# Token sums of an FFN on GpSimd, and one slot of row products moved to the end

## The chip, the cores and the metric

One core of a Trainium2 chip runs one launch of the kernel. The metric is the device time of the launch in microseconds, from repeated executions. The core's engines are TensorE (PE, matrix products), VectorE (DVE), ScalarE (ACT), GpSimd (POOL) and SyncE (SP), each with its own in-order queue; weights come by DMA.

## What is computed

A decoder trunk of two layers on 512 tokens of 1024 features, in float32. Layer 0 mixes tokens by dilated window attention, layer 1 by a gated linear recurrence. Each is followed by a gated FFN with a causal convolution of three taps; the change is in this part, which runs twice.

```python
D_MODEL = 1024; SEQ = 512; D_FF = 3 * D_MODEL

def conv_ffn(x, w_up, conv_w, conv_b, w_down):
    u = causal_dwconv(x @ w_up, conv_w, conv_b)
    g, v = u[..., :D_FF], u[..., D_FF:]
    return (jax.nn.gelu(g, approximate=True) * v) @ w_down

# in reference(), after the token mixer of each layer:
    h = rms_norm(x, norm_ffn_pre[layer])
    h = conv_ffn(h, ffn_w_up[layer], ffn_conv_w[layer], ffn_conv_b[layer], ffn_w_down[layer])
    x = x + rms_norm(h, norm_ffn_post[layer])
```

## The kernel before

**Precision.** Every operand of a product is kept as two float32r tiles, a high part `hi` (a rounding copy on ScalarE, L149) and a low part `lo` (the rest, a subtraction on VectorE, L150). A product is three matmuls: hi by hi, hi by lo, lo by hi (`PASSES`). The normed activations of a layer are `hT`, turned so that features lie on the partitions: two tiles of 128 x 8 x 512.

**An FFN.** `ffn` first takes the feature tiles of j = 0 and 1 as plain products (`feat_tiles`, `tiles`): 8 half tiles and 4 whole ones on TensorE, each followed by a tick. The other ten j (`SEVEN`) go through `seven`: for each j and each half (gate and value) one chain, twenty in all. A chain computes 256 features by seven block products in place of eight, from sums of blocks of weights on one side and of `hT` on the other. The sums of `hT` over halves of features and tokens are made once per FFN by `token_sums`: `both` adds hi and lo of a part of `hT` (L938, 128 x 512 elements), `whole` does it for the two parts of a block, the blocks `b11`, `b12`, `b22`, `b21` are combined on VectorE (L956, L963, L944) and split into the tiles `T[0]` to `T[3]` (`parted`).

**Slots.** A chain occupies a cycle of ten slots (`CYCLE`). `AT` says at which slot of its cycle a chain's step stands: step 1 at 0, 5 at 1, 2 at 2, 6 at 4, 3 at 5, 7 at 8, and 4 at 13, in the next chain's cycle. A step is twelve matmuls of 256 columns. Steps 5, 6, 7 and 4 multiply by `T[0]`, `T[1]`, `T[2]` and `T[3]`, the others by `hT`. A step accumulates in a PSUM bank that an earlier step wrote, so step 6 waits for the copy (L1031) of what step 1 left, step 3 for the copy after step 5, step 7 for the copy after step 6, and step 4 for an addition on VectorE that follows step 7 (L1040). The taps of the convolution are L777.

The slots that `free_slots` lists lie between the steps. They hold products of the second FFN matrix for the rows k = 0 to 19, two slots a row, six matmuls of 512 columns each (`rows`); with twenty chains there are forty. Slots that hold nothing are skipped.

**Order by hand.** The order on every engine is the order in which the program emits instructions. `slot` emits a step, then what is due (`later(n, f)` puts f behind n more slots), then `tick`: one step of every side generator, and `pump`, which converts the next weight piece to hi and lo (one piece per slot in `seven`, while at most 16 halves live). `token_sums` is such a side generator: each `yield n` lets n ticks pass. It is started five ticks into the FFN. `stream` lists the weight pieces of the chains by due times: the pieces `w11`, `s1`, `w12`, `s2`, `s3`, `s4`, `a22` of each chain, the additions between blocks of a weight tile (`left` and `ahead` as accumulating DMAs of GpSimd at L186, `across` at L210 and `lower` at L214 on VectorE), and for each row k its weight (`rows`, loaded by SyncE 16 slots before use) and its activation (`act`).

At its start `token_sums` also sends the residual stream to DRAM by a GpSimd DMA (L922), because its SBUF place becomes the home of `T`. The same function serves the attention stage with `first=True`, where it does not touch the residual stream.

Before an FFN the tokens are normed in four blocks t (`norms`, `prenorm`): products with gain and root on VectorE (L481, L485), transposition on TensorE (L502) and the split into `hT` (L506 on ScalarE, L507 on VectorE). The last block is still on its way when the first products of the FFN run.

Of the kernel before, what the change touches and what calls it, by code (L numbers as in the profile page):

```python
# [11 lines left out]
F32 = mybir.dt.float32  # L12
# [3 lines left out]
ALU = mybir.AluOpType  # L16
# [25 lines left out]
CYCLE = 10  # L42
# [41 lines left out]
def kernel(  # L84
# [25 lines left out]
    nc = tc.nc  # L110
# [12 lines left out]
    def nm(s):  # L123
        uid[0] += 1
        return f"{s}{uid[0]}"

    def gen(dt=F32, s="g"):
        return gp.tile([P, 512], dt, tag="g", name=nm(s))
# [19 lines left out]
    def split(hi, lo, raw):  # L148
        nc.scalar.activation(hi, raw, AF.Copy)  # L149
        nc.vector.tensor_tensor(lo, raw, hi.bitcast(F32), op=ALU.subtract)  # L150
# [41 lines left out]
    def free_slots(n):  # L192

        end = CYCLE * n
        free = [CYCLE * c + r for c in range(n) for r in ((6, 7) if c > 1 else (7,))] + [end, end + 1]
        assert not {CYCLE * c + a for c in range(n) for a in AT.values()} & set(free)
        return free

    def stream(i0, n):

        items = []
        for c in range(n):
# [15 lines left out]
            for at, item in (  # L218
# [4 lines left out]
                if isinstance(item[0], str):  # L223
                    item = ((i, item[0]), lambda i=i, h=item[1]: [blocks(i)[h]], item[0] == "a22")
                items.append((o + at, item))
        free = free_slots(n)
        direct = up["direct"]
        at = 0
# [535 lines left out]
    def ffn(layer, hT, post, pre):  # L764
# [63 lines left out]
        up["direct"] = direct  # L828
        T = []
        side(token_sums(hT, T), 5)  # L830
        for j in range(SEVEN[0]):
            if j:
# [84 lines left out]
    def token_sums(hT, T, first=False):  # L917

        if not first:
            assert len(sides) == 1, len(sides)  # L920
            d = dp.tile([P, 4, D], F32, name=nm("x_kept"))
            nc.gpsimd.dma_start(d, X[0])  # L922
            kept.append(d)
        homes = cp.tile([P, 4, D], F32R, tag="x_sb", name=nm("T"))
        homes = [homes[:, n] for n in range(4)]
        homes += [cp.tile([P, D], F32R, tag="gain", name=nm("T"), bufs=2) for _ in range(1 if first else 2)]
        homes = [[h[:, 0:512], h[:, 512:1024]] for h in homes]
        if first:
            homes += [[gen(F32R, "T") for _ in range(2)]]
        homes += [[wp.tile([P, 512], F32R, tag=t, name=nm("T")) for _ in range(2)] for t in ("hi", "lo")]  # L930
        state["live"] += 2
        homes = [[h.rearrange("p (k t) -> p k t", k=2) for h in hs] for hs in homes]
        yield 1 + first

        def both(k0, n):
            o = gen(s="B").rearrange("p (k t) -> p k t", k=2)
            hi, lo = (h[:, k0 : k0 + 2, n * 256 : n * 256 + 256] for h in hT)
            tt(o, hi.bitcast(F32), lo.bitcast(F32), op=ALU.add)  # L938
            return o

        tt = nc.vector.tensor_tensor

        def negative(o, a, b):
            nc.vector.scalar_tensor_tensor(o, a, -1.0, b, op0=ALU.mult, op1=ALU.subtract)  # L944

        def whole(k0, n):
            return [both(k0 + 2 * k, n) for k in range(2)]

        def parted(n, b):
            for k in range(2):  # L950
                split(homes[2 * n][k], homes[2 * n + 1][k], b[k])

        b11, b12 = whole(0, 0), whole(0, 1)
        yield 1 + first
        for k in range(2):
            tt(b11[k], b11[k], b12[k], op=ALU.subtract)  # L956
        parted(0, b11)
        yield 1 + first
        b22 = whole(4, 1)
        if not first:  # L960
            yield 1
        for k in range(2):
            tt(b12[k], b22[k], b12[k], op=ALU.subtract)  # L963
            negative(b22[k], b11[k], b22[k])
        yield 1 + first
        parted(1, b22)
        T.extend([homes[2 * n], homes[2 * n + 1]] for n in range(4))
        yield 1 + first
        parted(2, b12)
        yield 1 + first  # L970
        b21 = whole(4, 0)
        if first:
            yield 2
        for k in range(2):
            negative(b21[k], b22[k], b21[k])
        yield 1 + first
        parted(3, b21)
# [68 lines left out]
    def seven(hT, T, begin, prep):  # L1046
# [25 lines left out]
        for j in SEVEN:  # L1072
            for half in range(2):
                f = chain(right, *ends(j, half))
                steps.update((CYCLE * n + AT[p], f(p)) for p in AT)
                n += 1
        free = free_slots(n)
        assert len(free) == len(fill)
        steps.update(zip(free, fill))
# [12 lines left out]
    def attention(hT, post, pre):  # L1092
# [359 lines left out]
        for hp in range(4):  # L1452
            q, k = [], []
            if hp % 2 == 0:
                v = []
                values(v) if hp else first_values(v)
            if hp == 0:
                side(build)
                side(token_sums(hT, T, True), 2)
            sink = qk_sink(q, k)  # L1460
            if hp < 3:
                feat_tiles(2, hT, sink)
                for hh in range(2):
                    side(local(2 * hp + hh, hh, q, k, v), 1 + hh)
# [252 lines left out]
```

## Time and profile before

| | |
|---|---|
| median of 3 runs | 1430.48 us (1429.96 to 1431.25) |
| the profiled execution | 1431.97 us |
| its span, first to last instruction | 1430.1 us |
| mean granted clock of TensorE | 0.994 |
| busy: PE, DVE, ACT, POOL | 98%, 80%, 56%, 16% |
| plain products of the first FFN begin, its chains begin | 489.3 us, 535.9 us |
| the same in the second FFN | 1035.1 us, 1081.7 us |

Times in the profile are microseconds from the span's start, unless marked ns. A row of a timeline has the start, the duration, the engine, the line, the operation, what it writes and reads (by tile names, with buffer numbers left out), the form and the count, and in brackets the idle time of the engine ahead of it and what ended it. A row of the waits view has who waited and for whom, the sum, the number of times and the longest. The profile is one execution; matmul ends are modelled. Names ending in q are sequencers.

### The profile page before, as it was taken

The page shows a single profiled execution, that of the slowest core. Times are in us where ns is not written, and L with a number is a line of the kernel's source. Part 1 is how long each engine was busy: PE and PEld are TensorE (multiplying, and loading weights), DVE is VectorE, ACT ScalarE, POOL GpSimd, SP SyncE. Part 2 cuts the span into 40 slices and gives each one's busy share as a digit, 9 for nine tenths or more (in the row PEclk, how much of TensorE's full clock was granted, in tenths as well). Part 3 has the DMA queues.
Part 4 walks back from the last instruction along what each step waited for, and adds up shares of the span by engine and source line. Part 5 has one row for each costly group of instructions (what it writes and reads, how often), then busy time and mean ns, then how long its engine had stood idle before and what let it go on. Part 6 is the DMA issues. An engine that isn't in the chain of part 4 may idle for free.

```text
span 1430.1 us, 23824 instructions
## 1 busy us (share of the span) xinstructions
PE 1405.7 (98%) x8885; PEld 1275.0 (89%) x8885; DVE 1140.5 (80%) x2229; ACT 800.2 (56%) x1670; POOL 235.4 (16%) x352
## 2 busy tenths in 40 slices
PE   9999999999999998999999999999998999999997
PEld 7888999999998888999999889888897999999886
DVE  6676898787855988988888758779789898888843
ACT  7343555363636555666666555588455656666641
POOL 0341333130400211222110001000101112211000
PEclk9999999999999999999999999999999999999999
DMA  7553455664756545666664632432354666665511
GB/s 225 180 146 105 131 166 151 171 178 144 190 171 218 167 116 108 153 155 148 148 125 119 221 118 89 134 117 89 119 155 93 137 147 155 147 151 119 183 57 59
DMA packets 176108, 204.03 MB, mean 143 GB/s; under 512 B 10688, under 2 KB 145304, under 8 KB 175736
## 3 DMA queue, kind: packets, MB, share of 16 engines
q1 hardware_dynamic: 123064, 153.34, 33.5%
q0 software_dynamic: 52080, 48.11, 18.7%
q8 instruction: 70, 1.15, 0.3%
q10 hardware_dynamic: 848, 1.05, 0.2%
q14 instruction: 46, 0.38, 0.1%
HBM read 183.51 MB, written 18.96 MB: 142 GB/s over the span
## 4 chain that ended last, share of the span: by engine, by line
PE 84%; DVE 9%; ACT 5%; issue 1%; DMA 1%; POOL 0%; DVEq 0%; SPq 0%; ACTq 0%
PE ps L1022 38%; PE acc L412 24%; PE ps L412 9%; PE v L1215 7%; DVE wlo L150 2%; DVE u L777 2%; PE v L1153 1%; DVE xb L1520 1%; ACT whi L149 1%; PE O L1427 1%; PE S L1361 1%; PE S L1309 1%; DVE B L938 1%; ACT sig L1541 1%; PE tr L502 1%
## 5 line engine op out<-in xcount | busy, mean ns | idle before, releaser
L150 DVE TENSOR_TENSOR wlo<-raw,whi 128x512 fp32r<-128x512 f32 x632 | 417.5, 686 | 111.8 <-ACT whi L149 109.0
L149 ACT ACTIVATE whi<-raw 128x512 fp32r<-128x512 f32 x632 | 371.3, 625 | 141.9 <-PE ps L1022 45.9
L1022 PE MATMUL ps<-T,whi 128*128 128x256 f32 x1792 | 329.6, 284 | 14.8 <-ACT part L1031 11.0
L1022 PEld LDWEIGHTS ps<-T,whi 128*128 128x128 f32 x1792 | 280.6, 191 | 20.6 <-ACT part L1031 11.4
L1022 PE MATMUL ps<-T,wlo 128*128 128x256 f32 x896 | 252.0, 281 | 0.0
L1022 PE MATMUL ps<-hT,whi 128*128 128x256 f32 x1344 | 250.1, 284 | 0.0
L412 PE MATMUL ps<-hT,whi 128*128 128x512 f32 (+1 forms) x960 | 248.3, 348 | 0.0
L1022 PEld LDWEIGHTS ps<-hT,whi 128*128 128x128 f32 x1344 | 210.7, 192 | 0.8
L1022 PE MATMUL ps<-hT,wlo 128*128 128x256 f32 x672 | 190.9, 284 | 0.0
L412 PEld LDWEIGHTS ps<-hT,whi 128*128 128x128 f32 x960 | 167.6, 189 | 22.2
L186 POOL DMA_DIRECT2D raw<-in_ffn_w_up_dram x80 | 102.9, 1312 | 455.5 <-DVE wlo L150 337.2
L1022 PEld LDWEIGHTS ps<-T,wlo 128*128 128x128 f32 x896 | 171.5, 191 | 0.0
L412 PE MATMUL ps<-hT,wlo 128*128 128x512 f32 (+1 forms) x480 | 166.4, 347 | 0.0
L412 PE MATMUL acc<-whi,ahi 128*128 128x512 f32 x352 | 137.4, 390 | 0.0
L412 PE MATMUL acc<-whi,alo 128*128 128x512 f32 x352 | 137.2, 390 | 0.2
L412 PE MATMUL acc<-wlo,ahi 128*128 128x512 f32 x352 | 137.0, 389 | 0.0
L1022 PEld LDWEIGHTS ps<-hT,wlo 128*128 128x128 f32 x672 | 129.5, 193 | 0.0
L1031 ACT ACTIVATE part<-ps 128x256 f32<-128x256 f32 x168 | 63.8, 380 | 96.1 <-PE ps L1022 91.1
L1215 PE MATMUL v<-whi,hT 128*128 128x512 f32 x320 | 106.5, 396 | 0.0
L412 PEld LDWEIGHTS ps<-hT,wlo 128*128 128x128 f32 x480 | 90.8, 189 | 11.4
L777 DVE SCALAR_TENSOR_TENSOR u<-ps,cols,u 128x511 f32<-128x511 f32 x112 | 83.6, 746 | 4.9 <-ACT u L773 2.9
L773 ACT ACTIVATE u<-ps,cols 128x512 f32<-128x512 f32 x56 | 43.5, 776 | 70.8 <-DVE ps L1035 64.5
(206 smaller groups left out, 2165.3 us busy)
## 6 DMA issues: line engine op xcount, KB each, us to landing
raw<-in_ffn_w_up_dram SPq DMA_DIRECT2D x48, 1024.0 KB
raw<-in_attn_w_qkv_dram SPq DMA_DIRECT2D x67, 512.0 KB
raw<-in_ffn_w_up_dram POOLq DMA_DIRECT2D x80, 256.0 KB, 4.8
raw<-in_ffn_w_down_dram SPq DMA_DIRECT2D x14, 1024.0 KB
dw<-in_ffn_w_down_dram SPq DMA_DIRECT2D x40, 256.0 KB
raw<-in_lru_w_in_dram SPq DMA_DIRECT2D x8, 1024.0 KB
turned<-T POOLq DMA_DIRECT2D x26, 256.0 KB, 2.6
ft<-turned POOLq DMA_DIRECT2D x104, 64.0 KB, 4.4
```

Source lines behind the costliest of these rows:

```text
L149: nc.scalar.activation(hi, raw, AF.Copy)
L150: nc.vector.tensor_tensor(lo, raw, hi.bitcast(F32), op=ALU.subtract)
L186: nc.gpsimd.dma_start(to, src, accum_op=ALU.add)
L412: mm(dst, l[a], r[b], start=start and n == 0, stop=stop and n == 2)
L502: nc.tensor.transpose(ps[:, k * P : (k + 1) * P], xs[i][:, k * P : (k + 1) * P], ident)
L773: nc.scalar.activation(u, ps, AF.Identity, scale=own[:, j : j + 1], bias=cc[:, 48 + j : 49 + j])
L777: nc.vector.scalar_tensor_tensor(u[:, d:], ps[:, : S - d], wc, u[:, d:], op0=ALU.mult, op1=ALU.add)
L938: tt(o, hi.bitcast(F32), lo.bitcast(F32), op=ALU.add)
L1022: mm(dst, W[wa][0][:, k, :], right[n](ha, k), start=n in (1, 5) and k == q == 0, stop=k == 3 and q == 2, skip_group_check=True,)
L1031: later(1, lambda: nc.scalar.activation(to, dst, AF.Copy))
L1153: mm(banks[t], hT[a][:, k, t * P : (t + 1) * P], W[b][k % 2][:, 0, :], start=u == n == 0, stop=u == 3 and n == 5,)
L1215: mm(bank, hT[a][:, k, t * P : (t + 1) * P], W[b][k % 2][:, 0, :], start=(k, a, b) == (0, 0, 0), stop=(k, a, b) == (KD - 1, 1, 0),)
```

## The change

In `token_sums`, for the FFNs alone (`first` is false): all four blocks `b11`, `b12`, `b22`, `b21` are now added up at the generator's first step, and the eight additions run on GpSimd in place of VectorE, queued behind the DMA of L922. The generator's first `yield` and one later `yield` go, one becomes `yield 2`: the combinations of `b11` and `b12` keep their tick, all that follows comes one tick earlier. The attention stage keeps its order and engine.

In `free_slots`, the third cycle (slots 20 to 29) has one free slot in place of two, slot 27, and slot `end + 2`, which is 202, is added. The forty products of rows keep their order, so each from the third on takes the next slot of the list. The due times of the row weights and activations in `stream` are computed from the same list.

```diff
     def free_slots(n):
 
         end = CYCLE * n
-        free = [CYCLE * c + r for c in range(n) for r in ((6, 7) if c > 1 else (7,))] + [end, end + 1]
+        free = [CYCLE * c + r for c in range(n) for r in ((6, 7) if c > 2 else (7,))] + [end, end + 1, end + 2]
...
         homes = [[h.rearrange("p (k t) -> p k t", k=2) for h in hs] for hs in homes]
-        yield 1 + first
+        if first:
+            yield 2
 
         def both(k0, n):
             o = gen(s="B").rearrange("p (k t) -> p k t", k=2)
             hi, lo = (h[:, k0 : k0 + 2, n * 256 : n * 256 + 256] for h in hT)
-            tt(o, hi.bitcast(F32), lo.bitcast(F32), op=ALU.add)
+            (nc.vector if first else nc.gpsimd).tensor_tensor(o, hi.bitcast(F32), lo.bitcast(F32), op=ALU.add)
             return o
...
         b11, b12 = whole(0, 0), whole(0, 1)
-        yield 1 + first
+        if not first:
+            b22, b21 = whole(4, 1), whole(4, 0)
+        yield 2
         for k in range(2):
             tt(b11[k], b11[k], b12[k], op=ALU.subtract)
         parted(0, b11)
         yield 1 + first
-        b22 = whole(4, 1)
-        if not first:
-            yield 1
+        if first:
+            b22 = whole(4, 1)
         for k in range(2):
             tt(b12[k], b22[k], b12[k], op=ALU.subtract)
             negative(b22[k], b11[k], b22[k])
@@
         yield 1 + first
         parted(2, b12)
         yield 1 + first
-        b21 = whole(4, 0)
         if first:
+            b21 = whole(4, 0)
             yield 2
         for k in range(2):
             negative(b21[k], b22[k], b21[k])
```

## The prediction

> **What bounds the kernel now.** I read the page's busy times first, then the waits of TensorE, then the timelines around each wait.
>
> ```profile
> PE 1405.7 (98%) x8885; PEld 1275.0 (89%) x8885; DVE 1140.5 (80%) x2229; ACT 800.2 (56%) x1670; POOL 235.4 (16%) x352
> ...
> PE ps L1022 <- ACT part L1031: 11.0, 2, 5.5
> ...
> PE ps L1022 <- DVE ps L1040: 3.8, 3, 1.3
> ```
>
> TensorE is busy 98% of the span, so only its waits, or a slower clock, can be won. The waits view has two large ones: 5.5 us, twice, on a copy that ScalarE makes (L1031). Of the three on L1040, two lie in the stages that the change touches. TensorE's timeline shows the places:
>
> ```profile
> 545.78 0.80 PE L1022 MATMUL ps<-T,whi 128*128 128x256 f32 x2 [5.49 <-ACT part L1031]
> ...
> 552.05 0.39 PE L412 MATMUL acc<-whi,whi 128*128 128x512 f32 x1
> ...
> 552.74 0.40 PE L1022 MATMUL ps<-T,whi 128*128 128x256 f32 x2
> ...
> 799.05 0.39 PE L1022 MATMUL ps<-T,whi 128*128 128x256 f32 x1 [1.29 <-DVE ps L1040]
> ...
> 1091.61 0.80 PE L1022 MATMUL ps<-T,whi 128*128 128x256 f32 x2 [5.49 <-ACT part L1031]
> ...
> 1345.02 0.39 PE L1022 MATMUL ps<-T,whi 128*128 128x256 f32 x1 [1.28 <-DVE ps L1040]
> ```
>
> Each FFN shows the same pair: 5.49 us at slot 4 of the twenty chains (step 6 of the first chain), and 1.29 us before the very last step. The first one costs more than its length, as the windows view of L1022 tells (the stretch and its length, busy time and count of matmuls, the same of weight loads, granted clock, DMA share, GB/s):
>
> ```profile
> 545.77:551.70 5.93, 5.49 (x24) 5.20 (x24) 0.50 0.43 138
> ...
> 552.70:562.70 10.00, 9.96 (x84) 9.95 (x84) 1.00 0.91 199
> ```
>
> After the idle stretch the clock is 0.50. At clock 1.00 a matmul takes 10.00/84 = 0.119 us, a step of twelve 1.43 us; six row products take 2 x (552.74 - 552.05) = 1.38 us. From 545.78 to 552.74 there lie 24 step matmuls and six row products: 2 x 1.43 + 1.38 = 4.24 us at full clock, 6.96 measured. The slow clock costs 2.72 us, so that the wait costs 8.21 us per FFN. After the 1.29 us wait nothing of the kind is seen.
>
> What is late? ScalarE's timeline, then VectorE's:
>
> ```profile
> 513.89 0.62 ACT L149 ACTIVATE whi<-raw 128x512 fp32r<-128x512 f32 x1
> ...
> 514.42 0.76 ACT L773 ACTIVATE u<-ps,cols 128x512 f32<-128x512 f32 x1
> ...
> 543.70 1.23 ACT L149 ACTIVATE T<-B 128x512 fp32r<-128x512 f32 x2 [4.95 <-DVE B L944]
> ...
> 545.36 0.36 ACT L1031 ACTIVATE part<-ps 128x256 f32<-128x256 f32 x1
> ...
> 548.52 1.15 ACT L149 ACTIVATE whi<-raw 128x512 fp32r<-128x512 f32 x2 [2.00 <-DVE raw L210]
> ...
> 549.58 0.36 ACT L1031 ACTIVATE part<-ps 128x256 f32<-128x256 f32 x1
> ```
>
> ```profile
> 500.06 1.29 DVE L507 TENSOR_TENSOR hT<-tr,hT 128x512 fp32r<-128x512 f32 x2 [0.23 <-ACT hT L506]
> ...
> 501.27 3.69 DVE L150 TENSOR_TENSOR wlo<-raw,whi 128x512 fp32r<-128x512 f32 x6
> ...
> 506.43 1.53 DVE L777 SCALAR_TENSOR_TENSOR u<-ps,cols,u 128x511 f32<-128x511 f32 x2 [1.47 <-ACT u L773]
> ...
> 510.52 1.29 DVE L150 TENSOR_TENSOR wlo<-raw,whi 128x512 fp32r<-128x512 f32 x2 [2.56 <-ACT whi L149]
> ...
> 511.74 1.53 DVE L777 SCALAR_TENSOR_TENSOR u<-ps,cols,u 128x511 f32<-128x511 f32 x2
> ...
> 513.18 2.49 DVE L938 TENSOR_TENSOR B<-hT,hT 128x512 f32<-128x512 f32 x4
> ...
> 515.59 0.69 DVE L150 TENSOR_TENSOR wlo<-raw,whi 128x512 fp32r<-128x512 f32 x1
> ...
> 523.73 1.29 DVE L938 TENSOR_TENSOR B<-hT,hT 128x512 f32<-128x512 f32 x2
> ...
> 541.78 1.28 DVE L938 TENSOR_TENSOR B<-hT,hT 128x512 f32<-128x512 f32 x2
> ```
>
> The copy at 545.36 stands in ScalarE's queue behind the split of the fourth token sum (543.70), which waited 4.95 us for VectorE. From 511.74 on VectorE's rows show no idle time until the wait is over; four, two and two of the instructions in its queue are the adds of L938. The start is bound by VectorE's queue.
>
> **The adds leave VectorE.** Four adds hold it from 513.18 to 515.59, 2.41 us or 0.60 each; eight are 4.8 us. Not all of it comes through. Without the first four, VectorE would come at 513.18 to the low part (515.59), whose high part ScalarE ends at 513.89 + 0.62 = 514.51, and then to taps whose input ends at 514.42 + 0.76 = 515.18: about 1.4 us of idle time opens. Net, the queue runs 3.4 us earlier.
>
> **The token sums come a slot earlier.** With one yield less, the splits of the fourth sum no longer stand behind the last tile's taps and conversions, but the copy needed by step 7 (549.58) still stands behind a split that waits for L210. It gets the 3.4 us alone: it ends at 549.94 - 3.4 = 546.5. Where TensorE goes on at 545.78 - 5.49 = 540.29 without a wait at step 6, it stands before step 7 at 540.29 + 1.43 + 1.43 + 1.38 = 544.53. So the wait moves from step 6 to step 7 and is 2.0 us. I take the clock to stay at 1.00, since 2.0 is nearer to the 1.29 us row than to the 5.49 us row. Step 7 begins at 546.5 in place of 552.74: 6.2 us per FFN, which is the 8.2 of now less the 2.0 that remain.
>
> In the rule of the Trainium skill (TensorE: Matmul & The Clock Gate, Part 1: The HAM clock gate) the clock halves after about 3.4 us without work; by it too a wait of 2.0 us leaves the clock alone.
>
> **What GpSimd pays, and what it may take back.** No add of this size runs on GpSimd in this trace. Its own queue has room:
>
> ```profile
> 495.75 0.57 POOL L922 DMA_DIRECT2D x_kept<-x_sb  x1 [5.42 <-DVE x_sb L580]
> ...
> 516.57 2.63 POOL L186 DMA_DIRECT2D raw<-in_ffn_w_up_dram  x2 [20.25 <-DVE wlo L150]
> ...
> 531.22 2.58 POOL L186 DMA_DIRECT2D raw<-in_ffn_w_up_dram  x2 [12.02 <-DVE wlo L150]
> ...
> L1105 POOL COPY row<-rb 8x1 f32<-8x1 f32 x6 | 0.8, 177 | 0.1
> ...
> L1105 POOL COPY row<-rb 8x30 f32<-8x30 f32 x2 | 0.4, 201 | 0.0
> ```
>
> The adds are queued between 495.75 and 516.57, ahead of the accumulating DMAs that wait for VectorE anyhow. Two may begin at 496.3, as the first half of the tokens is complete; the others wait for the last tokens (500.06 + 1.29 = 501.35). A copy costs 24/29 = 0.83 ns an element, so an add of 512 costs 0.60 us if both reads go side by side, 1.03 us if one follows the other; as an estimate from these rows I take 1.03, and 2.06 as the upper end. Six adds from 501.35 end by 507.5, or 513.7: ahead of the first use, which VectorE reaches at about 517 (518.36 now):
>
> ```profile
> 518.36 1.28 DVE L956 TENSOR_TENSOR B<-B,B 128x512 f32<-128x512 f32 x2
> ...
> 530.24 1.29 DVE L150 TENSOR_TENSOR wlo<-raw,whi 128x512 fp32r<-128x512 f32 x2
> ```
>
> So GpSimd's slowness itself costs nothing. What may cost is work of VectorE beside it. Where GpSimd issues DMAs (531.22), VectorE's pair at 530.24 takes the usual 1.29 us, so the lower end is 0. The upper end is that the six low parts from 501.27, each reading two SBUF tiles, wait for an add in turn: five adds between six instructions, 5 x 1.03 less the 1.47 us idle row behind them, 3.7 us per FFN. Another collision can come earlier:
>
> ```profile
> 497.54 0.88 DVE L485 TENSOR_SCALAR xs<-xs,s 128x512 f32<-128x512 f32 x2
> ...
> 498.80 0.38 PE L502 MATMUL tr<-ident,xs 128*128 128x128 f32 x2
> ```
>
> These scalings end 0.4 us before TensorE transposes their results, and the first two adds would run beside them. I take 1.0 us per FFN in all, one add's hold-up: nearer to the DMA row than to the alternation.
>
> **The moved slot.** Six matmuls move from slot 26 to slot 202; their count is unchanged. At the end, TensorE gets 1.38 us of work between slots 201 and 203, while what step 4 waits for (L1040, behind step 7 at slot 198) does not move. That covers the 1.29 us. In the third cycle eight steps then follow as closely as they already do in the first two, where, besides step 6, the waits view shows nothing. From slot 27 on each weight conversion is issued one slot later against its use: the shortest lead, that of s4, goes from seven slots to six, over 8 us. The order of conversions stays: row weights and activations still lie between s2 and s3 of their chain, though L214 now precedes them and the SP loads of the row weights come one slot later, fifteen slots before use. One more half lives (14 of 16). I cost this at nothing; the leads hide it, and if they did not, each late slot would show as a TensorE wait.
>
> **Sum.** Per FFN: -6.2 (start) - 1.3 (end) + 1.0 (GpSimd beside VectorE) = -6.5 us; two FFNs, -13.0 us. The profiled execution took 1431.97 us, a span of 1430.1 and 1.9 around it; it would take 1419.0. It stood 1.5 us above the median of 1430.48, so the forecast is **1417.5 us**.
>
> **Rivals.**
>
> *VectorE and GpSimd alternate.* Every two-tile instruction of VectorE waits for the add in flight. The queue is late by 3.7 us; step 6 waits 3.7 and step 7 2.0. Per FFN -8.2 + 5.7 - 1.3 = -3.8, in all -7.6: 1422.9 us. For it: six such instructions lie just where the adds run. Against: no row shows GpSimd's work stretching one. Chance 0.25.
>
> This is the rule of the Trainium skill (SBUF — State Buffer, Who interferes with whom): an instruction of VectorE with two SBUF inputs and a GpSimd instruction that reads SBUF exclude each other for the whole instruction; no overlap of the two is in this trace. GPSIMD Engine Reference, Performance versus the Vector engine, states 4497 ns for 2048 elements, an estimate of 1.1 to 1.25 us for 512; with 1.25 the sum by this rival would be near 1426.5.
>
> *The same, with slow adds: slower.* With an add of length a, step 6 waits 5a - 1.47, and where that is near 5.49 again the clock falls too (+2.72), whose slower steps hide the wait at step 7. Against 8.21 + 1.29 it breaks even at a = (8.21 + 1.29 - 2.72 + 1.47)/5 = 1.65 us. At the upper end, 2.06, it is 8.83 + 2.72 - 9.50 = +2.05 per FFN, +4.1: 1434.6 us. Chance 0.12.
>
> *The start does not gain.* The copy stays behind ScalarE work that follows TensorE's tiles, not VectorE, and the adds bring nothing; the end slot alone gives -2.6: 1427.9 us. Against it: the 4.95 us row names VectorE. Chance 0.08.
>
> **How the numbers follow.** My own case has 0.52, and 0.03 is left for others. A measurement can tell some 0.2%, 2.9 us, from no change. Faster: 0.52 + 0.25 + 0.02 = 0.79; same: 0.08 + 0.01 = 0.09; slower 0.12. The range goes from 1414.5 (no collision at all, -15.0, and a little more at step 7) to 1428.0, which holds the alternation and the end slot alone, and leaves out the slower case.
>
> **What would show it.** Right: eight adds on GpSimd per FFN, in the first one between 496 and 512, no L938 on VectorE but the first stage's eight; no 5.49 us wait, one of about 2 us at step 7; clock 1.00 throughout; no L1040 wait at the ends. Wrong: the six low parts after 501 spread over 8 us or more; a wait of over 4 us with the clock at 0.50; or new TensorE waits from the third cycle on.

## The result: no change that can be measured

| | before | after |
|---|---|---|
| median, lowest and highest of 12 runs each | 1430.56 us (1429.51 to 1433.91) | 1430.45 us (1430.00 to 1431.60) |
| ratio after to before, 95% interval | | 0.9998 (0.9989 to 1.0007) |
| profiled execution, its span | 1431.97 us, 1430.1 us | 1430.45 us, 1428.7 us |

The forecast was 1417.5 us. In the profile after, step matmuls are L1024, the copy that step 6 waits for is L1033, the addition behind step 7 is L1042, and all additions of `both` are L939. First the page's busy times and the waits of TensorE:

```profile
PE 1405.0 (98%) x8885; PEld 1273.9 (89%) x8885; DVE 1147.4 (80%) x2213; ACT 800.4 (56%) x1670; POOL 260.0 (18%) x368
...
PE ps L1024 <- ACT part L1033: 10.3, 3, 4.9
PE tr L502 <- DVE xs L485: 3.3, 2, 1.7
...
PE ps L1024 <- DVE ps L1042: 1.1, 1, 1.1
```

Two readings. VectorE has 16 instructions fewer than before (2213 against 2229) and is busy 6.9 us longer (1147.4 against 1140.5). Sixteen additions of 0.60 us, 9.7 in all, left it, so the others grew by 16.6 us; where an instruction that is held up counts as busy, that is how a hold-up looks. And the long wait is still there, shorter by little, with a new one of 1.7 us on the scalings L485. Of the waits on the addition behind step 7, the two at the ends of the FFNs are gone; the one left lies in the attention stage. TensorE's timeline:

```profile
500.42 1.09 PE L502 MATMUL tr<-ident,xs 128*128 128x128 f32 x8 [1.66 <-DVE xs L485]
...
546.86 0.79 PE L1024 MATMUL ps<-T,whi 128*128 128x256 f32 x2 [4.88 <-ACT part L1033]
...
553.86 0.40 PE L1024 MATMUL ps<-T,whi 128*128 128x256 f32 x2
...
1092.50 0.79 PE L1024 MATMUL ps<-T,whi 128*128 128x256 f32 x2 [4.88 <-ACT part L1033]
...
1098.92 0.50 PE L1024 MATMUL ps<-T,whi 128*128 128x256 f32 x2 [0.55 <-ACT part L1033]
```

Step 7 begins at 553.86, where it began at 552.74. The windows view has the slow clock behind the wait as before. Its columns here: the stretch and its length; busy time and count of TensorE, its weight loads, VectorE, ScalarE and GpSimd; granted clock, DMA share, GB/s:

```profile
546.86:550.20 3.34, 3.34 (x15) 3.34 (x16) 3.34 (x6) 0.74 (x2) 0.00 (x0) 0.50 0.00 0
550.30:553.69 3.39, 3.39 (x16) 3.12 (x16) 3.29 (x7) 1.43 (x3) 1.02 (x1) 0.62 0.39 103
```

Then what GpSimd and VectorE did at the FFN's start. GpSimd's timeline, its group of additions over both FFNs, and VectorE's timeline:

```profile
495.56 0.57 POOL L922 DMA_DIRECT2D x_kept<-x_sb  x1 [5.40 <-DVE x_sb L580]
496.14 2.55 POOL L939 TENSOR_TENSOR B<-hT,hT 128x512 f32<-128x512 f32 x2
502.84 9.80 POOL L939 TENSOR_TENSOR B<-hT,hT 128x512 f32<-128x512 f32 x6 [4.15 <-DVE hT L507]
...
L939 POOL TENSOR_TENSOR B<-hT,hT 128x512 f32<-128x512 f32 x16 | 24.7, 1576 | 8.3 <-DVE hT L507 8.3
```

```profile
495.18 0.68 DVE L481 TENSOR_TENSOR xs<-x_sb,gain 128x512 f32<-128x512 f32 x1
...
496.03 3.21 DVE L481 TENSOR_TENSOR xs<-x_sb,gain 128x512 f32<-128x512 f32 x1
...
499.87 0.88 DVE L485 TENSOR_SCALAR xs<-xs,s 128x512 f32<-128x512 f32 x2
...
500.88 2.48 DVE L507 TENSOR_TENSOR hT<-tr,hT 128x512 fp32r<-128x512 f32 x4
503.28 9.92 DVE L150 TENSOR_TENSOR wlo<-raw,whi 128x512 fp32r<-128x512 f32 x6
513.12 1.52 DVE L777 SCALAR_TENSOR_TENSOR u<-ps,cols,u 128x511 f32<-128x511 f32 x2
```

The six low parts, 3.69 us before, take 9.92 beside six additions. The additions too are held up: the first two, beside which VectorE's product stood still, take 2.55 us, 1.3 each, but six take 9.80, so from one to the next it is (9.80 - 1.30) / 5 = 1.70 us. The two engines take turns. Earlier, the product L481 takes 3.21 us: it stood through both of the first additions. Before, its row was this:

```profile
496.23 0.68 DVE L481 TENSOR_TENSOR xs<-x_sb,gain 128x512 f32<-128x512 f32 x1
```

L777 comes at 513.12, where it came at 506.43.

To set the runs side by side, three distances, read from TensorE's timeline in both FFNs: from the start of the first transposition to that of the last one ("norms"), from there to the start of step 7 of the first chain ("start"), from there to the end of the twenty chains ("chains"). The first FFN stands ahead of the second.

| | norms | start | chains | median, us |
|---|---|---|---|---|
| before | 16.6, 16.6 | 53.2, 53.3 | 248.0, 248.0 | 1430.56 |
| after | 18.5, 18.5 | 52.6, 52.0 | 246.5, 246.6 | 1430.45 |

The norms lose 1.9 us per FFN, the start gains 0.6 and 1.3, the chains gain 1.5 and 1.5. Together that is -1.1 us; the span shrank by 1.4.

### The profile page after: what moved, and what is told of

Same layout as the page of the kernel before. It is cut to its first block, busy times and chain, and to the rows that moved or that the text cites. A ratio compares the mean times of both kernels' runs of the same rounds, so it can differ in the third digit from the quotient of the medians.

```text
span 1428.7 us, 23886 instructions
## 1 busy us (share of the span) xinstructions
PE 1405.0 (98%) x8885; PEld 1273.9 (89%) x8885; DVE 1147.4 (80%) x2213; ACT 800.4 (56%) x1670; POOL 260.0 (18%) x368
## 4 chain that ended last, share of the span: by engine, by line
PE 48%; DVE 11%; ACT 5%; issue 2%; DMA 0%; DVEq 0%; ACTq 0%
PE ps L1024 27%; PE acc L412 20%; DVE wlo L150 3%; DVE xb L1522 1%; DVE u L777 1%; ACT whi L149 1%; PE ps L412 1%; ACT sig L1543 1%; DVE x_sb L580 1%; DVE post L575 1%; DVE T L150 1%; DVE hT L507 0%; ACT sig L1562 0%; ACT a L1560 0%; ACT xhi L149 0%
## 5 line engine op out<-in xcount | busy, mean ns | idle before, releaser
L150 DVE TENSOR_TENSOR wlo<-raw,whi 128x512 fp32r<-128x512 f32 x632 | 432.2, 705 | 125.2 <-ACT whi L149 121.0
L1024 PE MATMUL ps<-T,whi 128*128 128x256 f32 x1792 | 329.5, 284 | 11.4 <-ACT part L1033 10.3
L1024 PEld LDWEIGHTS ps<-T,whi 128*128 128x128 f32 x1792 | 280.7, 191 | 16.9 <-ACT part L1033 11.1
L1024 PE MATMUL ps<-T,wlo 128*128 128x256 f32 x896 | 252.0, 281 | 0.0
L1024 PE MATMUL ps<-hT,whi 128*128 128x256 f32 x1344 | 249.3, 284 | 0.0
L1024 PEld LDWEIGHTS ps<-hT,whi 128*128 128x128 f32 x1344 | 210.0, 192 | 0.8
L1024 PE MATMUL ps<-hT,wlo 128*128 128x256 f32 x672 | 190.4, 283 | 0.0
L1024 PEld LDWEIGHTS ps<-T,wlo 128*128 128x128 f32 x896 | 171.5, 191 | 0.0
L1024 PEld LDWEIGHTS ps<-hT,wlo 128*128 128x128 f32 x672 | 129.0, 192 | 0.0
L1033 ACT ACTIVATE part<-ps 128x256 f32<-128x256 f32 x168 | 63.4, 378 | 79.2 <-PE ps L1024 78.3
L777 DVE SCALAR_TENSOR_TENSOR u<-ps,cols,u 128x511 f32<-128x511 f32 x112 | 83.5, 745 | 2.0
L455 POOL DMA_DIRECT2D turned<-T x34 | 18.6, 549 | 350.3 <-DVE T L449 348.7
```

The source lines that it names most:

```text
L455: nc.gpsimd.dma_start(d, T)
L777: nc.vector.scalar_tensor_tensor(u[:, d:], ps[:, : S - d], wc, u[:, d:], op0=ALU.mult, op1=ALU.add)
L1024: mm(dst, W[wa][0][:, k, :], right[n](ha, k), start=n in (1, 5) and k == q == 0, stop=k == 3 and q == 2, skip_group_check=True,)
L1033: later(1, lambda: nc.scalar.activation(to, dst, AF.Copy))
```

## The experiments

Theory A is the forecast's rival of alternation: an instruction of VectorE with two tiles from SBUF and an addition on GpSimd exclude each other. Theory B: the moved slot costs in the third cycle what it gains at the end. Theory C: ScalarE or TensorE's tiles hold the start, whoever adds. Theory D: any work of GpSimd holds up VectorE. The code cuts are against the kernel after, except that of e9_fill, which is against the kernel before. Line numbers below an edit differ from run to run: the copy that step 6 waits for stands nine lines below the step matmuls, the addition behind step 7 eighteen.

**e1_slot: the slot alone.** The change with `token_sums` as before, all its yields included.

```diff
-        if first:
-            yield 2
+        yield 1 + first
...
-            (nc.vector if first else nc.gpsimd).tensor_tensor(o, hi.bitcast(F32), lo.bitcast(F32), op=ALU.add)
+            tt(o, hi.bitcast(F32), lo.bitcast(F32), op=ALU.add)
...
```

> The slot moved alone, the additions on VectorE as before. Theory A (two reads exclude each other: a VectorE instruction that reads two SBUF tiles and a GpSimd addition cannot run at the same time, and what the moved slot wins is lost by this): the wait of 1.29 us before the last step goes in both FFNs, the 5.49 us wait stays, 2.6 to 3.2 us faster than before. Rival B (the moved slot itself costs in the third cycle what it wins at the end): no faster than before, and a new TensorE wait behind slot 27.

Measured: 1428.32 us, ratio 0.9983 (0.9974 to 0.9992). The waits view keeps the start as before and has no wait at the ends:

```profile
PE ps L1022 <- ACT part L1031: 11.0, 2, 5.5
...
PE ps L1022 <- DVE ps L1040: 1.1, 1, 1.1
```

The chains take 246.5 us in both FFNs, as after. The median fell by 2.2 us; the expected 2.6 to 3.2 lies within the interval (1.1 to 3.7 us). The slot does what was forecast, and theory B falls.

**e2_adds: the additions alone.** The change with `free_slots` as before.

```diff
-        free = [CYCLE * c + r for c in range(n) for r in ((6, 7) if c > 2 else (7,))] + [end, end + 1, end + 2]
+        free = [CYCLE * c + r for c in range(n) for r in ((6, 7) if c > 1 else (7,))] + [end, end + 1]
```

> The additions on GpSimd alone, the slots as before. Theory A: the two waits at the transposition (1.7 us) and the wait at step 6 (4.9 us, clock at 0.50 behind it) as with the whole change, and the 1.29 us at the end again: 2 to 3.5 us slower than before. Rival B: 0 to 3 us faster than before.

Measured: 1433.72 us, ratio 1.0024 (1.0014 to 1.0034). The waits at the start are those of after, those at the ends are back:

```profile
PE ps L1024 <- ACT part L1033: 10.4, 3, 4.9
PE tr L502 <- DVE xs L485: 3.4, 2, 1.7
PE ps L1024 <- DVE ps L1042: 3.2, 3, 1.3
```

So the two parts of the change have opposite signs, +3.2 and -2.2 us by the medians, and hide each other up to about a microsecond.

**e4_none: no additions.** The change with the eight additions left out, so that the sums are made from the high parts alone.

```diff
...
-            (nc.vector if first else nc.gpsimd).tensor_tensor(o, hi.bitcast(F32), lo.bitcast(F32), op=ALU.add)
+            if not first:
+                return hi.bitcast(F32)
+            nc.vector.tensor_tensor(o, hi.bitcast(F32), lo.bitcast(F32), op=ALU.add)
...
```

> The whole change, but the eight additions of each FFN are left out: the sums are made from the high parts alone, so the low parts are missing in them; every other instruction stays. Theory A, and the forecast's own assumption of additions that disturb nothing: one wait of about 2 us at step 7, clock 1.00, 14 to 16 us faster than before. Rival C (the start is held by ScalarE's queue behind TensorE's tiles, so the additions never mattered): a wait of about 5 us stays, only 2.6 to 3.2 us faster than before.

Measured: 1417.69 us, ratio 0.9912 (0.9898 to 0.9925). TensorE's timeline and VectorE's:

```profile
546.31 0.50 PE L1036 MATMUL ps<-T,whi 128*128 128x256 f32 x2 [1.85 <-ACT part L1045]
```

```profile
501.20 3.69 DVE L150 TENSOR_TENSOR wlo<-raw,whi 128x512 fp32r<-128x512 f32 x6
506.36 1.53 DVE L777 SCALAR_TENSOR_TENSOR u<-ps,cols,u 128x511 f32<-128x511 f32 x2 [1.47 <-ACT u L773]
```

No wait at step 6, one of 1.85 us at step 7, which begins at 546.31. With the additions gone the start gains what the forecast said, so ScalarE does not hold it: theory C falls. The median fell by 12.8 us, where 14 to 16 was expected; the profiled execution, 1416.53 us, lies 15.4 under that of before, and the four times reach up to 1420.21, a spread that comes up again with e10_idle.

**e5_memset: GpSimd busy, but reading nothing.** In place of each addition three writes of a constant; the token sums are left out.

```diff
-            (nc.vector if first else nc.gpsimd).tensor_tensor(o, hi.bitcast(F32), lo.bitcast(F32), op=ALU.add)
+            if first:
+                nc.vector.tensor_tensor(o, hi.bitcast(F32), lo.bitcast(F32), op=ALU.add)
+            else:
+                for _ in range(3):
+                    nc.gpsimd.memset(o, 0.0)
```

> The whole change, but in place of each addition GpSimd runs three memsets of the same tile, which write SBUF and read nothing; the sums are zero. GpSimd is busy from about 496 to 509 us, as long as with the additions. Theory A: the six low parts behind 501 us take 3.7 us as before, the products with the gain 0.7 us; at most the scalings L485, the only kind there that runs faster than one element a cycle, are held up; 11 to 16 us faster than before. Rival D (any work of GpSimd beside VectorE holds it up, reading or not): the six low parts take 8 us or more, and the time is within 3 us of before.

Measured: 1419.54 us, ratio 0.9919 (0.9905 to 0.9933). GpSimd's timeline and VectorE's:

```profile
496.33 13.59 POOL L943 MEMSET B<- 128x512 f32 x24
```

```profile
496.25 0.68 DVE L481 TENSOR_TENSOR xs<-x_sb,gain 128x512 f32<-128x512 f32 x1
...
497.56 1.52 DVE L485 TENSOR_SCALAR xs<-xs,s 128x512 f32<-128x512 f32 x2
...
501.88 3.69 DVE L150 TENSOR_TENSOR wlo<-raw,whi 128x512 fp32r<-128x512 f32 x6
```

GpSimd is busy for 13.6 us (with additions 2.55 and 9.80), and beside it L481, with its two tiles, takes its 0.68 us and the six low parts their 3.69. So writing does not exclude instructions with two tiles, and for them theory D falls. It does not fall altogether: the scalings L485, with one tile in and one out, take 1.52 us in place of 0.88 beside the writes.

**e12_copy: GpSimd reads one tile.** Each addition replaced by a copy of the high part; the low parts of the sums are left out.

```diff
-            (nc.vector if first else nc.gpsimd).tensor_tensor(o, hi.bitcast(F32), lo.bitcast(F32), op=ALU.add)
+            if first:
+                nc.vector.tensor_tensor(o, hi.bitcast(F32), lo.bitcast(F32), op=ALU.add)
+            else:
+                nc.gpsimd.tensor_copy(o, hi.bitcast(F32))
```

> The change, with each of the eight additions on GpSimd replaced by a copy of its high part: one tile read in place of two; the low parts of the sums are left out. Theory A in its narrow form (any read of GpSimd excludes VectorE's instructions with two tiles): the six low parts alternate with copies, each some 0.6 us plus the copy's own length, and take 7 us or more in place of 3.69; the time lies between the kernel without additions and the change, some 1420 to 1427 us. Rival (only two reads of GpSimd exclude): 3.69 us, no wait above 2 us, about 1418 us.

Measured: 1418.58 us, ratio 0.9915 (0.9900 to 0.9930). GpSimd's timeline and VectorE's:

```profile
495.96 1.18 POOL L942 COPY B<-hT 128x512 f32<-128x512 f32 x2
500.22 4.77 POOL L942 COPY B<-hT 128x512 f32<-128x512 f32 x6 [3.08 <-ACT hT L506]
```

```profile
495.88 1.81 DVE L481 TENSOR_TENSOR xs<-x_sb,gain 128x512 f32<-128x512 f32 x1
...
499.33 2.48 DVE L507 TENSOR_TENSOR hT<-tr,hT 128x512 fp32r<-128x512 f32 x4
501.73 5.01 DVE L150 TENSOR_TENSOR wlo<-raw,whi 128x512 fp32r<-128x512 f32 x6
```

One tile read is enough: L481 stands through both copies (1.81 us), and the low parts take 5.01 us. The time alone would have spoken for the rival: 1418.58 us is its 1418, and lies under the 1420 to 1427 expected by theory A. The rows decide, since by the rival nothing would have been held up. The expected 7 us was too much, because a copy needs only the high part of the tokens and starts at 500.22: the first ones ran beside L507, which reads one tile from PSUM and one from SBUF, and which kept its time (2.48 us for four). The 1.3 us that the low parts lost go into the idle time ahead of L777 (1.47 us in e4_none), so the start is only 0.3 to 0.4 us longer than there.

**e6_order: no early additions.** The two additions that need the last tokens are issued first.

```diff
-        b11, b12 = whole(0, 0), whole(0, 1)
-        if not first:
+        if first:
+            b11, b12 = whole(0, 0), whole(0, 1)
+        else:
+            b12, b11 = whole(0, 1), whole(0, 0)
             b22, b21 = whole(4, 1), whole(4, 0)
```

> The change with the additions on GpSimd in another order: the two that need the last tokens first, so that none runs ahead of them. Theory A: the wait of 1.66 us at the transposes goes and the scaling takes 0.68 us again; the six low parts still alternate with additions over some 10 us and TensorE's long wait stays, with the clock at 0.50 behind it: about 1427 us. Rival (the early pair is the whole loss): the long wait goes too and the time is near 1418 us.

Measured: 1425.95 us, ratio 0.9969 (0.9957 to 0.9980). GpSimd's timeline, VectorE's, and the waits:

```profile
500.47 12.78 POOL L939 TENSOR_TENSOR B<-hT,hT 128x512 f32<-128x512 f32 x8 [4.51 <-DVE hT L507]
```

```profile
500.90 9.94 DVE L150 TENSOR_TENSOR wlo<-raw,whi 128x512 fp32r<-128x512 f32 x6
```

```profile
PE ps L1026 <- ACT part L1035: 9.7, 3, 4.6
```

The norms are back at 16.6 us, 3.7 less over both FFNs, and the median stands 4.5 us under that of after: about that much is the early collision's part. The other stays, with the low parts at 9.94 us and waits of 4.6 us.

**e3_vector: new places, VectorE.** One word of the change undone.

```diff
-            (nc.vector if first else nc.gpsimd).tensor_tensor(o, hi.bitcast(F32), lo.bitcast(F32), op=ALU.add)
+            nc.vector.tensor_tensor(o, hi.bitcast(F32), lo.bitcast(F32), op=ALU.add)
```

> The whole change with one word undone: the eight additions are issued at the new places but to VectorE. Theory A: no exclusion; the additions fill the 2.56 us of idle time ahead of the first taps and cost the queue some 2.3 us against the kernel without additions. TensorE's waits at the start of the twenty chains add up to about 4.1 us per FFN: about 1422 us if the clock stays up, 1428 if it falls. Rival (the order of issue, not GpSimd, costs the time): no better than the change, 1430 us.

Measured: 1421.0 us, ratio 0.9938 (0.9926 to 0.9951). VectorE's timeline and TensorE's:

```profile
510.20 4.90 DVE L939 TENSOR_TENSOR B<-hT,hT 128x512 f32<-128x512 f32 x8
515.02 1.29 DVE L150 TENSOR_TENSOR wlo<-raw,whi 128x512 fp32r<-128x512 f32 x2
```

```profile
544.70 0.50 PE L1024 MATMUL ps<-T,whi 128*128 128x256 f32 x2 [2.09 <-ACT part L1033]
...
551.12 0.50 PE L1024 MATMUL ps<-T,whi 128*128 128x256 f32 x2 [1.91 <-ACT part L1033]
```

Waits of 4.0 us in all, as expected. In the second FFN the clock fell behind the first of them (2.07 us there), but the slower steps only shortened the second one to 0.40 us, and the start is as long as in the first FFN. On VectorE the eight additions cost 4.90 us of queue and the start is 2.4 us longer than without any; on GpSimd it is 5.8 and 5.2 us longer. The same work costs less on the busier engine.

**e9_fill: the price of the slow clock.** The kernel before, with matmuls in the wait.

```diff
+            if m == 4:
+                acc[0] = psum("acc")
+                for _ in range(18):
+                    mm(acc[0], hT[0][:, 0, :P], hT[0][:, 0, :], start=True, stop=True)
             if m in steps:
                 slot(steps[m])
```

> The kernel before, with 18 matmuls of 512 columns (4.1 us) whose result nobody reads put ahead of step 6, into the wait of 5.49 us. If the slow clock behind the wait costs what the prediction put on it (2.72 us per FFN), TensorE waits some 1.4 us there, the clock stays at 1.00 and the time falls by about 5.4 us to 1425. Rival: the slow steps only hide other waits, and the time stays at 1430.

Measured: 1426.31 us, ratio 0.9971 (0.9961 to 0.9982). TensorE's timeline and the windows view:

```profile
545.40 0.51 PE L1022 MATMUL ps<-T,whi 128*128 128x256 f32 x2 [1.39 <-ACT part L1031]
```

```profile
545.40:549.70 4.30, 4.30 (x30) 3.99 (x31) 4.20 (x8) 2.17 (x5) 0.69 (x1) 1.00 0.21 45
```

The copy is no earlier, but the clock stays at 1.00. The start takes 50.6 us in both FFNs, 2.6 and 2.7 less than before: what the prediction put on the slow clock, 2.72. The median moved by 4.2 us in place of 5.4; the interval (2.6 to 5.6 us) holds both.

**e10_idle: additions in VectorE's idle time.** The moved slot, and all additions on VectorE: those of `b11` as the generator starts, which is a tick earlier, those of `b12` and `b22` a tick later, those of `b21` one more.

```diff
-        side(token_sums(hT, T), 5)
+        side(token_sums(hT, T), 4)
...
+            b11 = whole(0, 0)
+            yield 1
...
+            b12, b22 = whole(0, 1), whole(4, 1)
+            yield 1
+            b21 = whole(4, 0)
+            yield 1
```

> The moved slot stays; all eight additions go back to VectorE, but each pair into a stretch where VectorE was idle: the first pair as soon as the first half of the tokens stands, two pairs in the cycle after, the last in the cycle behind that. Exclusion of two reads (theory A): GpSimd reads no tiles any more, the six low parts take 3.69 us and the scaling of the last tokens 0.68, and most of the additions' 4.8 us falls into idle time: about the time of the kernel without additions, 1418 to 1422 us. Rival: VectorE has no idle time that counts, its queue is as late as before by the additions and only the end slot gains, near 1428 us.

Measured: 1418.9 us (1417.16 to 1420.35), ratio 0.9921 (0.9907 to 0.9934). VectorE's timeline and the windows behind the wait of 1.91 us at step 7 of both FFNs:

```profile
503.23 1.29 DVE L924 TENSOR_TENSOR B<-hT,hT 128x512 f32<-128x512 f32 x2
...
507.44 2.49 DVE L924 TENSOR_TENSOR B<-hT,hT 128x512 f32<-128x512 f32 x4
...
512.74 1.28 DVE L924 TENSOR_TENSOR B<-hT,hT 128x512 f32<-128x512 f32 x2
```

```profile
546.18:549.60 3.42, 3.42 (x28) 3.42 (x29) 2.98 (x5) 2.05 (x4) 0.67 (x1) 1.00 1.04 334
1084.55:1087.90 3.35, 3.35 (x16) 3.35 (x17) 2.98 (x5) 1.99 (x4) 0.67 (x1) 0.52 1.03 335
```

All eight are there, and the start takes 47.1 us, 0.2 to 0.3 more than without any. The gain sought from GpSimd was to be had by order alone. Behind the same wait the clock stayed up in one FFN and fell in the other; there the chains take 248.1 us in place of 246.6, so this fall cost 1.5 us (e5_memset has it in both FFNs, behind 1.93 us).

**e11_idlefill: the same, with the last wait filled.**

```diff
+            if m == 8:
+                acc[2] = psum("acc")
+                for _ in range(8):
+                    mm(acc[2], hT[0][:, 0, :P], hT[0][:, 0, :], start=True, stop=True)
             if m in steps:
                 slot(steps[m])
```

> The kernel with the additions in VectorE's idle stretches, and eight matmuls of 512 columns (1.8 us), whose result nobody reads, ahead of step 7, into the wait of 1.91 us that is left there. If the wait costs only its length plus, in some executions, a slow clock of 3.4 us (1.7 us lost), the wait falls to about 0.1 us, step 7 begins no later, the clock stays at 1.00 in both FFNs and the time is 1417, with a narrower spread than the 1417.2 to 1420.4 without them. Rival: the slow clock there costs nothing, and the time stays at 1419.

Measured: 1417.04 us (1416.70 to 1417.65), ratio 0.9905 (0.9888 to 0.9921). The windows from step 7 on:

```profile
546.36:549.80 3.44, 3.44 (x28) 3.44 (x29) 2.98 (x5) 2.07 (x4) 0.66 (x1) 1.00 1.06 330
1084.75:1088.20 3.45, 3.45 (x29) 3.45 (x30) 2.98 (x5) 2.09 (x4) 0.66 (x1) 1.00 1.03 329
```

No wait is left in the FFNs, and the clock stays up in both. The spread is 1.0 us in place of 3.2, which fits falls of 1.5 us that come or do not; the ratios of the two kernels overlap, so that the smaller median is not shown to be a gain. By the medians both kernels beat before and after by 11 to 14 us, 2.2 of it by the moved slot (e1_slot).

The three distances in all runs:

| | norms | start | chains | median, us |
|---|---|---|---|---|
| e1_slot | 16.6, 16.6 | 52.5, 52.1 | 246.5, 246.5 | 1428.32 |
| e2_adds | 18.5, 18.5 | 52.1, 52.6 | 248.1, 248.0 | 1433.72 |
| e3_vector | 16.6, 16.6 | 49.2, 49.2 | 246.6, 246.6 | 1421.00 |
| e4_none | 16.6, 16.6 | 46.8, 46.8 | 246.6, 246.6 | 1417.69 |
| e5_memset | 16.6, 16.6 | 47.1, 47.1 | 248.1, 248.1 | 1419.54 |
| e6_order | 16.6, 16.6 | 51.7, 52.4 | 246.6, 246.5 | 1425.95 |
| e9_fill | 16.6, 16.6 | 50.6, 50.6 | 248.0, 248.0 | 1426.31 |
| e10_idle | 16.6, 16.6 | 47.1, 47.1 | 246.6, 248.1 | 1418.90 |
| e11_idlefill | 16.6, 16.6 | 47.1, 47.1 | 246.6, 246.6 | 1417.04 |
| e12_copy | 17.1, 17.1 | 47.2, 47.2 | 246.6, 246.6 | 1418.58 |

## Why the prediction failed

**What bounds the start: right.** It named VectorE's queue, not ScalarE. Without additions (e4_none) the wait at step 6 is gone, one of 1.85 us stands at step 7 (forecast 2.0), and the start shortens by 6.4 and 6.5 us (forecast 6.2).

**The end slot: right.** The chains gain 1.5 us per FFN with the slot and nothing without it; the forecast said 1.3.

**"What GpSimd pays, and what it may take back": here it failed.** The term was 1.0 us per FFN, "nearer to the DMA row than to the alternation". That row shows GpSimd busy, and e5_memset shows that GpSimd can be busy for 13.6 us without holding up an instruction of two tiles: a busy row was no evidence on an instruction that reads. In place of 1.0 came two hold-ups, 7.7 and 7.1 us in the two FFNs. The norms lengthened by 1.9 us per FFN: of the early collision the text saw the scalings and their 0.4 us of lead, not the product L481 ahead of them. And the low parts took 6.2 us longer (9.92 less 3.69), with the start 5.8 and 5.2 us above e4_none, slow clock included.

**The rival of alternation: the mechanism, with the wrong size.** Its formula, low parts' delay less the idle 1.47 us, gives 6.23 - 1.47 = 4.8 us for the wait at step 6; 4.88 was measured. But it took 3.7 from an addition of 1.03 us, guessed from small copies. An addition took 1.30 alone, and the turns come at 1.70. With 4.8 the wait is long enough for the slow clock, which the forecast had put into the slower rival only. That rival's own sum, with 4.8 for its term, is 4.8 + 2.72 - 9.50 = -2.0 us per FFN; with the +1.9 of the norms it is -0.1, close to what was seen. So the two rivals together had the terms of the start, and neither came to zero without the loss in the norms. That gain and loss cancel so nearly is a coincidence of sizes. One figure of the prediction does not belong where it stands: for an addition of 1.25 us this rival's own sum is 4.78 + 2.0 - 8.2 - 1.3 = -2.7 per FFN, or 1425.0 us; the 1426.5 has the slow clock of the next rival in it.

The rule of the Trainium skill that the prediction named (SBUF — State Buffer, Who interferes with whom) agrees with these runs in both halves: a GpSimd instruction that reads SBUF excluded those with two SBUF inputs (0.68 us to 3.21), one that only writes did not (0.68 in e5_memset). The rule deserved more than the chance of 0.25.

**The clock.** Taken to stay at 1.00 behind 2.0 us: not reliably so. Behind waits of 1.91 to 2.09 us the traces show both, and a fall cost 1.5 us in e10_idle. The rule of the Trainium skill (TensorE: Matmul & The Clock Gate, Part 1: The HAM clock gate), some 3.4 us without work, is not what e10_idle shows, whose clock fell behind 1.91 us. What went with a fall can be worked out from the clock records of the twelve traces. Within each trace all changes of the clock lie whole multiples of 3.413 us apart (in e10_idle it rose at 6.07, fell at 1084.68 and rose at 1088.10: 316 and 1 of them). On that grid, five waits of 1.89 to 2.07 us had 1.89 us or more inside one interval, and the clock fell at the end of it; of the waits that a boundary cut, with at most 1.84 us on one side, none of up to 2.09 us lost it. So the wait of 1.91 us in e10_idle cost nothing in the FFN where it was cut in two, and 1.5 us in the other.

## What to carry to other kernels

Before work goes to GpSimd, list what VectorE does in the same stretch: here what had two tiles from SBUF was held up by instructions of GpSimd that read one or two, the low parts to 5.01 us by copies and to 9.92 by additions, in place of 3.69. Look for idle stretches in the busy engine's own queue first; here they held all eight additions for 0.2 to 0.3 us of delay per FFN, where the idle engine cost 5 to 6. And a sum of two edits that comes out at zero is two questions: each edit run alone had an effect that could be measured.

## What the runs showed of the hardware

- An addition of 128 x 512 elements takes 1.30 us on GpSimd, 0.61 on VectorE (4.90 / 8 in e3_vector); a copy takes 0.6 us on GpSimd (1.18 for two).
- A held instruction counts as busy: L481 at 3.21 us, the low parts at 1.65 on average (9.92 / 6). VectorE's busy time rose by 6.9 us though sixteen additions were taken off it.
- Turns are not always fair: L481 stood through two additions (3.21 us) and through two copies (1.81 us), while low parts and additions alternated one by one. By the trace L481 began at 496.03, ahead of the first addition at 496.14, and still came last. What decides that was not tried.
- An instruction of VectorE with one tile from PSUM and one from SBUF kept its time beside GpSimd's copies (L507, 2.48 us for four).
- GpSimd's writes alone slowed VectorE's scalings of one tile (0.88 to 1.52 us for two).
- TensorE's clock fell to half for 3.4 us or more behind all waits of 4.6 us and over that were seen in the FFNs, behind none of up to 1.85 us there, and behind some of 1.91 to 2.09 us. The one fall in the attention stage came behind 1.89 us (e3_vector). All these falls came at the end of an interval of a 3.413 us grid in which TensorE had waited 1.89 us or more; up to 1.84 us in one interval there was none.
